# A two-layer decoder trunk: residual stream laid out by tokens, with weights as the moving operand of the output projections

## Chip, core and metric

The kernel runs on one core of one Trainium2 chip. The metric is the device time of one execution in microseconds (us). The engines are TensorE (PE in the profile, with PEld for its weight loads), VectorE (DVE), ScalarE (ACT), GpSimd (POOL) and SyncE (SP), whose queue issues the DMAs.

## What is computed

512 tokens of width 1024 go through two layers. Each layer has a token mixer (a gated DeltaNet in layer 0, forgetting attention, "fox", in layer 1), four heads of attention to 256 memory rows beside it, an output projection and a squared-ReLU MLP. Everything is float32.

```python
def rms_norm(x, w):
    y = x * lax.rsqrt(jnp.mean(x * x, axis=-1, keepdims=True) + EPS)
    return y * w
for i in range(2):
    h = rms_norm(x, norm1_w[i])
    mix, q_mem = gated_deltanet(h, ...) if i == 0 else forgetting_attention(h, ...)
    mem_out = memory_attention(q_mem, mem_k, mem_v, memq_norm_w[i])
    x = x + jnp.concatenate([mix, mem_out], axis=-1) @ w_out[i]      # 1536 -> 1024
    h = rms_norm(x, norm2_w[i])
    x = x + jnp.square(jax.nn.relu(h @ w_mlp1[i])) @ w_mlp2[i]       # 1024 -> 4096 -> 1024
```

In forgetting attention the projections q, k, v and gate are 1024 wide each (8 heads of 128); q and k are normalised per head.

## The kernel before

Every float32 operand of a large product is cut into a rounded part ("hi") and the rest ("lo"). `mm3` (L156 to L160) makes three products of them: hi hi, hi lo, lo hi. The weights come in slabs of 512 KB (1024 rows by 256 columns, or 512 rows by 512 columns): a DMA brings the raw slab, ACT casts it to the hi part (L297), DVE subtracts to get the lo part (L298). `prepare` does this some slabs ahead.

**Layout.** From the output projection of layer 0 on, the residual stream x is feature-major: 8 blocks of 128 features by 512 tokens (`x_blk`). `rows512` (L1278) makes x += w part for one slab of 512 weight rows and 512 columns: for each block of 128 output features 12 products, in which 128 weight columns are stationary and the 512 tokens of the input are the moving operand; then DVE adds the PSUM tile to the block of x (L1287). The output projection is three such groups (memory heads, then heads 0 to 3, then 4 to 7), the second half of the MLP eight.

**Norms.** Since x has features on partitions, the sum of squares of a token runs across partitions. For each finished block `split` (ACT L396, DVE L397) multiplies by the norm's weight and writes hi and lo of the next input hT at once, without the token's scale; `add_sq` squares the block (ACT L407) and POOL adds it to `sqs` (L408). After the last block, products of `ones` with `sqs` (L165) give the sums, twelve small DVE operations (L373, L208 to L212, L374) the rsqrt, and `r_row` spreads it along the free axis by 4 transposes (L170). So products on hT can start before the scale is known; the scale is applied when results leave PSUM: in the MLP's `hidden` (L1302, then the square on POOL L1303, the cast on ACT L1304, the lo part on DVE L1305), in the copies of layer 1's mixer (L1225, L467) and in the gate (L1248).

**MLP.** The hidden layer is 8 groups of 512. `m1(g, s)` makes 256 hidden columns from a slab (48 products with 512 tokens moving, `gemm_feat`). Groups alternate: m1(g, 0), half of the second product of group g-1, m1(g, 1), the other half.

**Layer 1's mixer.** First a 264-wide product (8 forget logits and 256 columns of memory queries, L1211), then four pairs of heads. For each pair k, q and v come by `gemm_tok2`: token-major tiles [128 tokens, 256], with hT as the stationary operand and 256 weight columns moving, 24 products for each of 4 tiles; the gate is feature-major (`gemm_feat`, 48 products of 512). k and q are normalised per head in the background (`group_scale`: POOL L444, DVE L445, DVE small operations, POOL L450; then transposes in `heads_T2`), and `self.drain("qk")` after the gate waits in the program for both.

**Order.** There is one instruction stream per engine, fixed when the program is built. Side work (norms, head attention) is written as generators in lanes; each `yield` says how much TensorE work in ns shall stand before the next step, and `pump` puts the steps between the products of the main stream. A `drain` emits the steps of a lane at once. Nothing is reordered on the chip: each engine works off its own list and waits on semaphores.

Of the kernel before, what the change touches and what calls it, by code (L numbers as in the profile page):

```python
# [7 lines left out]
F32 = mybir.dt.float32  # L8
# [22 lines left out]
# columns of the packed per-partition parameters  # L31
# [7 lines left out]
PC_N = 110  # L39
NPC = 134  # L40


class Kern:
# [68 lines left out]
    # A step yields how much TensorE work (in ns) goes before its results are used.  # L112
# [28 lines left out]
    def drain(self, *names, until=None):  # L141
        """Traces the lanes by their times until the named ones are at their ends, or until a mark is set."""
# [12 lines left out]
    def mm3(self, out, l, r, start, stop):  # L155
        """float32 product through the exact parts: hi hi + hi lo + lo hi."""  # L156
# [46 lines left out]
    def rsqrt(self, v, n):  # L203
        """v: AP [P, n] (with its guard added); returns v ** -0.5."""
# [10 lines left out]
    def log1p_half(self, u, n):  # L215
        """u in (0, 1]: log(1 + u) / 2 = atanh(u / (2 + u))."""
# [23 lines left out]
    def plan_weights(self):  # L240
# [42 lines left out]
    def prepare(self, n, cuts=1, also={}):  # L283
        """Splits slabs of the plan; if self.help, GpSimd takes half of the subtractions."""
# [20 lines left out]
    def slab(self, ahead=1):  # L305
        """The next slab of the plan: a function (k, columns) -> its hi and lo parts."""
# [11 lines left out]
    def gemm_feat(self, hT, evac, blk0=0, need=None):  # L318
        """Two feature-major blocks [128, 512] of hT's projection."""
# [10 lines left out]
    def gemm_tok(self, hT, evac, N=512, ns=2, nt=NT, by_tile=False, need=None):  # L330
        """Token-major [128, N] for each tile of tokens; ns slabs of 512 rows."""
# [3 lines left out]
        for s in range(1 if by_tile else ns):  # L335
            w = None if by_tile else self.slab()
            ks = range(K) if by_tile else range(4 * s, 4 * s + 4)
            order = [(k, t) for t in range(nt) for k in ks] if by_tile else [(k, t) for k in ks for t in range(nt)]
            for k, t in order:
                if need and (k if by_tile else t) == 0:  # L340
                    self.drain(until=need(t if by_tile else k))
# [5 lines left out]
    def gemm_tok2(self, hT, evac):  # L347
        """Token-major [128, 256] for each tile of tokens; one slab of 256 columns."""
        w = self.slab()
        for t in range(NT):  # L350
            ps = self.pacc()[:, :256]
            for k in range(KC):
                self.mm3(ps, hT(k, slice(t * P, t * P + P)), w(k), k == 0, k == KC - 1)
            evac(t, ps)
# [11 lines left out]
    def sq_sums(self, sqs, n, r):  # L366
        """r[:, i] = rsqrt(mean + eps) of the tokens of column block i of sqs [P, n * 128], summed over partitions."""
        nc = self.nc
        ps = self.paux3()
        for i in range(n):  # L370
            self.mm(ps[:, i], sqs[:, i * P:(i + 1) * P], self.ones)
        v = self.small(n)
        nc.vector.tensor_scalar(v, ps[:, :n, 0], 1.0 / D, EPS, ALU.mult, ALU.add)  # L373
        nc.vector.tensor_copy(r, self.rsqrt(v, n))  # L374

    def r_row(self, r):
        """The norm's scale of each token along the free axis, on all partitions; a generator."""
        nc = self.nc
        rb = self.scr3()
        nc.vector.tensor_copy(rb, self.bc(r, P))  # L380
        yield 1090.0
        ps = self.paux3()
        for t in range(NT):
            self.tr(ps[:, t], rb[:, t])
        self.rrow = self.cst.tile([P, T], F32, tag="rrow", name=self.nm("rrow"))
        nc.scalar.copy(self.rrow, ps.rearrange("p a b -> p (a b)"))

    def n_col(self, i, b):
        return self.par[:, PC_N + 8 * (i - 1) + b:PC_N + 8 * (i - 1) + b + 1]

    def split(self, hT, b, v, i):
        """v [P, T], times norm i's weight, into the parts of block b of hT."""
        nc = self.nc
        hi, lo = hT(b)
        w = self.n_col(i, b)
        nc.scalar.activation(hi, v, AF.Copy, scale=w)  # L396
        nc.vector.scalar_tensor_tensor(lo, v, w, hi.bitcast(F32), ALU.mult, ALU.subtract)  # L397

    def add_sq(self, b, xb):
        """Adds block b's squares to the norm's sums."""  # L400
        nc = self.nc
        if b == 0:
            self.sqs = self.cst.tile([P, T], F32, tag="sqs", name=self.nm("sqs"))
            nc.scalar.activation(self.sqs, xb, AF.Square)
        else:
            sq = self.scr()
            nc.scalar.activation(sq, xb, AF.Square)  # L407
            nc.gpsimd.tensor_add(self.sqs, self.sqs, sq)  # L408

    def norm_end(self, name):  # L410
        yield 2800.0
        self.r = self.cst.tile([P, NT], F32, tag="r", name=self.nm("r"))
        self.sq_sums(self.sqs, NT, self.r)
        self.marks.add("r" + name)
        yield 5520.0
        yield from self.r_row(self.r)
        self.marks.add("row" + name)
# [20 lines left out]
    def group_scale(self, raw, n, mult, eps):  # L438
        """raw [P, n, 128], scaled in place by rsqrt(mult * sum of squares + eps) of each group."""
# [13 lines left out]
    def heads_T(self, raw, dst, wcol, nt=NT):  # L453
        """raw [P, nt * 4, 128] (tile, head) -> dst [P, 4 heads, nt * 128], times a weight per row."""
# [8 lines left out]
    def cut2(self, parts, v, w):  # L463
        """v times a weight per row, into its hi and lo parts."""
# [4 lines left out]
    def heads_T2(self, raw, parts, wcol):  # L469
        """raw [P, 4 tiles * 2 heads, 128] -> the parts [P, 2 heads, T] of its transpose, times a weight per row."""  # L470
# [12 lines left out]
    def load_x(self, src):  # L483
        self.xs = [self.slot(T) for _ in range(2)]
        for b in range(0, KC, 2):
# [944 lines left out]
```

## Time and profile before

| | us |
|---|---|
| three runs | 1460.39, 1461.47, 1464.43 |
| their median | 1461.47 |
| span of the profiled execution | 1458.1 |
| PE busy in it | 1433.3 (98%) |
| DVE, ACT, POOL busy | 895.9, 584.1, 361.9 |

The span runs from the first to the last instruction; the median of the runs lies 3.4 us above it. A profile row of an engine's timeline gives start, duration, engine, line and operation, out<-in with shapes, and in brackets the idle time before it with what released it. Products overlap in the PE, so the distance from start to start says what one costs in a dense stream, not its duration.

### The profile page before, as it was taken

What the parts mean: (1) busy time and instruction counts of PE and PEld (TensorE: products, weight loads), DVE (VectorE), ACT (ScalarE), POOL (GpSimd) and SP (SyncE); (2) the same over time, 40 slices, a digit from 0 to 9 for tenths busy, and PEclk for the clock granted to TensorE, in tenths of its full rate; (3) what the DMA queues carried; (4) which work ended last, traced back from release to release, by engine and by line L of the source; (5) the groups of instructions that cost most, each with busy time, mean ns of one, the idle gap of its engine ahead of it and who ended that gap; (6) DMA issues with size and microseconds to landing.
All of it is one profiled execution on the core that took longest, in us unless ns stands there. A gap on an engine that the chain in (4) does not pass through costs nothing.

```text
span 1458.1 us, 20510 instructions
## 1 busy us (share of the span) xinstructions
PE 1433.3 (98%) x7886; PEld 1221.3 (84%) x7886; DVE 895.9 (61%) x1660; ACT 584.1 (40%) x1024; POOL 361.9 (25%) x406
## 2 busy tenths in 40 slices
PE   8999999989999999999999999999999999999999
PEld 6988777878888888888889999999888888888887
DVE  7689987577665554554566756657656545545544
ACT  7464655654342222222234554554534222222221
POOL 2274233223031111111122443444313101101100
PEclk9999999999999999999999999999999999999999
DMA  7541231232223223223335232213323322322331
GB/s 249 171 148 59 67 114 61 72 123 88 84 91 102 91 98 101 95 93 101 98 99 168 72 103 86 89 66 122 132 87 102 101 93 84 113 98 85 107 101 59
DMA packets 49783, 148.35 MB, mean 102 GB/s; under 512 B 5459, under 2 KB 10259, under 8 KB 49429
## 3 DMA queue, kind: packets, MB, share of 16 engines
q1 hardware_dynamic: 49536, 146.96, 30.8%
q8 instruction: 62, 1.02, 0.3%
q14 instruction: 37, 0.30, 0.1%
q10 hardware_dynamic: 148, 0.07, 0.0%
HBM read 139.64 MB, written 7.37 MB: 101 GB/s over the span
## 4 chain that ended last, share of the span: by engine, by line
PE 82%; DVE 9%; DMA 2%; ACT 2%; issue 2%; POOL 2%; ACTq 0%; SPq 0%; POOLq 0%; DVEq 0%
PE acc L158 25%; PE acc L159 24%; PE acc L160 24%; PE aux L165 3%; PE aux L170 2%; DVE wl L298 2%; DVE cv L751 2%; PE aux L160 1%; PE aux L158 1%; PE aux L159 1%; DVE slot L830 1%; ACT wh L297 1%; DMA t<-gd 1%; DVE slot L828 1%; POOL t L930 0%
## 5 line engine op out<-in xcount | busy, mean ns | idle before, releaser
L158 PE MATMUL acc<-slot,wh 128*128 128x512 f32 x1476 | 579.8, 393 | 0.0
L159 PE MATMUL acc<-slot,wh 128*128 128x512 f32 x1476 | 574.7, 389 | 0.3 <-DVE slot L1269 0.3
L160 PE MATMUL acc<-slot,wl 128*128 128x512 f32 x1476 | 574.4, 389 | 0.0
L297 ACT ACTIVATE wh<-wr 128x1024 fp32r<-128x1024 f32 (+3 forms) x242 | 247.6, 1025 | 494.4 <-PE acc L159 456.7
L298 DVE TENSOR_TENSOR wl<-wr,wh 128x1024 fp32r<-128x1024 f32 (+3 forms) x240 | 299.2, 1249 | 217.9 <-ACT wh L297 213.5
L160 PEld LDWEIGHTS acc<-slot,wl 128*128 128x128 f32 x1476 | 277.1, 188 | 57.7
L158 PEld LDWEIGHTS acc<-slot,wh 128*128 128x128 f32 x1476 | 277.2, 188 | 55.1
L159 PEld LDWEIGHTS acc<-slot,wh 128*128 128x128 f32 x1476 | 277.4, 188 | 54.7 <-DVE slot L1269 0.6
L1303 POOL TENSOR_TENSOR cv<-cv 128x512 f32<-128x512 f32 x64 | 94.7, 1501 | 536.7 <-DVE cv L1302 523.3
L158 PE MATMUL acc<-wh,slot 128*128 128x256 f32 (+3 forms) x608 | 187.7, 310 | 1.4 <-ACT slot L509 0.8
L159 PE MATMUL acc<-wl,slot 128*128 128x256 f32 (+3 forms) x608 | 183.8, 302 | 0.9 <-POOL wl L298 0.7
L160 PE MATMUL acc<-wh,slot 128*128 128x256 f32 (+3 forms) x608 | 182.9, 302 | 0.0
L1287 DVE TENSOR_TENSOR slot<-slot,acc 128x512 f32<-128x512 f32 x177 | 120.5, 681 | 96.1 <-PE acc L160 95.9
L158 PEld LDWEIGHTS acc<-wh,slot 128*128 128x128 f32 x608 | 116.3, 191 | 7.1 <-ACT slot L509 2.4
L159 PEld LDWEIGHTS acc<-wl,slot 128*128 128x128 f32 x608 | 116.4, 191 | 6.0 <-DVE wl L298 1.4
L160 PEld LDWEIGHTS acc<-wh,slot 128*128 128x128 f32 x608 | 115.9, 191 | 3.8
L1302 DVE SCALAR_TENSOR_TENSOR cv<-acc,rrow 128x512 f32<-128x512 f32 x64 | 43.7, 691 | 80.0 <-PE acc L160 80.0
L1305 DVE TENSOR_TENSOR slot<-cv,slot 128x512 fp32r<-128x512 f32 x64 | 69.7, 1090 | 6.9 <-ACT slot L1304 2.4
L1304 ACT CAST slot<-cv 128x512 fp32r<-128x512 f32 x64 | 39.8, 622 | 58.4 <-POOL cv L1303 58.4
L751 DVE SCALAR_TENSOR_TENSOR cv<-acc,par,cv 128x511 f32<-128x511 f32 (+2 forms) x72 | 51.4, 740 | 16.0 <-ACT cv L748 15.6
L408 POOL TENSOR_TENSOR sqs<-sqs,cv 128x512 f32<-128x512 f32 x21 | 28.8, 1369 | 108.8 <-ACT cv L407 108.8
L444 POOL TENSOR_TENSOR cv<-slot 128x512 f32<-128x512 f32 x26 | 31.0, 1197 | 57.8 <-ACT slot L1225 30.7
(249 smaller groups left out, 1348.7 us busy)
## 6 DMA issues: line engine op xcount, KB each, us to landing
wr<-in_w_mlp SPq DMA_DIRECT2D x128, 512.0 KB, 3.8
wr<-in_w_out SPq DMA_DIRECT2D x24, 512.0 KB, 4.3
wr<-in_dn_k SPq DMA_DIRECT2D x8, 512.0 KB, 4.8
wr<-in_dn_v SPq DMA_DIRECT2D x8, 512.0 KB, 4.6
wr<-in_dn_q SPq DMA_DIRECT2D x8, 512.0 KB, 3.6
wr<-in_dn_z SPq DMA_DIRECT2D x8, 512.0 KB, 4.0
wr<-in_fox_k SPq DMA_DIRECT2D x8, 512.0 KB, 4.1
wr<-in_fox_q SPq DMA_DIRECT2D x8, 512.0 KB, 3.7
```

The costliest lines, as they stand in the source:

```text
L158: mm(out, l[0], r[0], start=start, stop=False)
L159: mm(out, l[0], r[1], start=False, stop=False)
L160: mm(out, l[1], r[0], start=False, stop=stop)
L165: self.nc.tensor.matmul(out, l, r, start=start, stop=stop)
L297: nc.scalar.activation(hi[:, c], raw[i][:, c], AF.Copy)
L298: eng.tensor_sub(lo[:, c], raw[i][:, c], hi[:, c].bitcast(F32))
L751: nc.vector.scalar_tensor_tensor(y[:, s:], ps[:, :T - s], w(j), y[:, s:], ALU.mult, ALU.add)
L1287: self.nc.vector.tensor_add(xv, xv, ps)
L1302: nc.vector.scalar_tensor_tensor(r, ps, 0.0, self.rrow, ALU.max, ALU.mult)
L1303: nc.gpsimd.tensor_mul(r, r, r)
L1304: nc.scalar.copy(hh[:, b, :], r)
L1305: nc.vector.tensor_sub(hl[:, b, :], r, hh[:, b, :].bitcast(F32))
```

## The change

x becomes token-major: 4 tiles of 128 tokens by 1024 features (`x_tile`), and the output leaves the kernel that way. In the output projections and second MLP matrices (`tile_add`) 128 tokens of the input are stationary and 512 weight columns move. The last group of each takes both slabs and goes by pairs of tiles (`rows_last`), so that `norm_tile` can start on a tile when its 1024 features are there: two squares with a sum on ACT, 13 small DVE operations per tile, two DVE multiplications by scale and weight (in `transposed`), 8 PE transposes, ACT copies for hi and DVE subtractions for lo. hT now has the scale, so the evictions lose their multiplications; in `hidden` ACT does the ReLU and DVE the square. The first MLP group of each layer works on 2 slabs at once, in halves of 256 tokens (`gemm_halves`), the second half needing tiles 2 and 3. The 264-wide product of layer 1 goes by tiles. k and q of a pair come from one slab pair 512 wide, v for two pairs at once.

```diff
-                    pl += [a["fox_" + n][p] for p in (2 * g, 2 * g + 1) for n in "kqvg"]
+                    for p in (2 * g, 2 * g + 1):
+                        pl += tok(a["fox_kq"][p])
+                        if p % 2 == 0:
+                            pl += tok(a["fox_v"][g])
+                        pl += [a["fox_g"][p]]
...
+    def gemm_halves(self, hT, evac, need):
+        w = [self.slab(), self.slab(0)]
+        ps = [self.pacc() for _ in range(4)]
+        for i in range(2):
+            c = slice(256 * i, 256 * i + 256)
+            for t in range(2 * i, 2 * i + 2):
+                self.drain(until=need(t))
+            for j in range(2):
+                for k in range(KC):
+                    for b in range(2):
+                        self.mm3(ps[2 * j + b][:, c], w[j](k, slice(b * P, b * P + P)), hT(k, c), k == 0, k == KC - 1)
+        for b in range(4):
+            evac(b, ps[b])
...
+    def stats(self, tiles, r):
+        nc = self.nc
+        for i, xt in enumerate(tiles):
+            s2 = self.small(2)
+            for f in range(2):
+                jk = self.scr()
+                nc.scalar.activation(jk, xt[:, f * 512:(f + 1) * 512], AF.Square, accum_out=s2[:, f:f + 1])
+            nc.vector.tensor_add(r[:, i:i + 1], s2[:, 0:1], s2[:, 1:2])
+        nc.vector.tensor_scalar(r, r, 1.0 / D, EPS, ALU.mult, ALU.add)
+        nc.vector.tensor_copy(r, self.rsqrt(r, len(tiles)))
...
+    def norm_weight(self, i):
+        w = self.cst.tile([P, D], F32, tag="nw", name=self.nm("nw"))
+        self.nc.sync.dma_start(w, self.a["norms"][i].partition_broadcast(P))
+        return [w[:, g * 512:(g + 1) * 512] for g in range(2)]
+    def norm_tile(self, i, t, hT, w, spill=None):
+        yield 700.0
+        xt = self.x_tile(t)
+        r = self.small(1)
+        self.stats([xt], r)
+        if spill is not None:
+            self.nc.sync.dma_start(spill[t], xt)
+        yield 3600.0
+        yield from self.transposed(xt, w, r, hT.parts, t)
+        self.marks.add(f"h{i}{t}")
...
-        self.gemm_tok(hT, e0, N=264, need=lambda k: f"h2{k}")
+        self.gemm_tok(hT, e0, N=264, by_tile=True, need=lambda t: f"h2{t}")
...
+            def e(t, ps, rv=rv):
+                nc.scalar.copy(rv[:, :, t, :], ps.rearrange("p (j c) -> p j c", j=2))
+            self.gemm_tok(hT, e)
...
-                self.gemm_tok2(hT, e)
...
             if p % 2 == 0:
+                vh, vl = self.slot(512, F32R), self.slot(512, F32R)
+                def e(t, ps, vh=vh, vl=vl):
+                    nc.scalar.copy(vh[:, t, :], ps)
+                    nc.vector.tensor_sub(vl[:, t, :], ps, vh[:, t, :].bitcast(F32))
+                self.gemm_tok(hT, e)
                 gate = self.slot(T)
...
-                nc.vector.tensor_mul(gv, ps, self.rrow)
-                nc.scalar.activation(gv, gv, AF.Sigmoid)
+                nc.scalar.activation(gv, ps, AF.Sigmoid)
...
+    def tile_add(self, t, f, part, w, c=slice(0, 512)):
+        ps = self.pacc()[:, c]
+        for k in range(4):
+            self.mm3(ps, tuple(m[:, t * P:t * P + P] for m in part(k)), w(k, c), k == 0, k == 3)
+        xv = self.x_tile(t)[:, f * 512 + c.start:f * 512 + c.stop]
+        self.nc.vector.tensor_add(xv, xv, ps)
...
+    def rows_last(self, part, after, last=False):
+        w = [self.slab(), self.slab(0)]
+        for i in range(2):
             for f in range(2):
+                for t in (2 * i, 2 * i + 1):
+                    cut = [slice(0, 256), slice(256, 512)] if last and i and f and t % 2 else [slice(0, 512)]
+                    for c in cut:
+                        self.tile_add(t, f, part, w[f], c)
+                        if last:
+                            after(t, slice(f * 512 + c.start, f * 512 + c.stop))
+                    if f and not last:
+                        after(t)
...
-            nc.vector.scalar_tensor_tensor(r, ps, 0.0, self.rrow, ALU.max, ALU.mult)
-            nc.gpsimd.tensor_mul(r, r, r)
+            nc.scalar.activation(r, ps, AF.Relu)
+            nc.vector.tensor_mul(r, r, ps)
             nc.scalar.copy(hh[:, b, :], r)
             nc.vector.tensor_sub(hl[:, b, :], r, hh[:, b, :].bitcast(F32))
...
-        m1(0, 0, lambda k: f"h{name}{k}")
-        m1(0, 1)
+        self.gemm_halves(hT, lambda b, ps: hidden(0, b, ps), lambda t: f"h{name}{t}")
```

The built programs differ as follows: products 512 wide into `acc` go from 4692 to 5076, products 256 wide from 1368 to 600, PE transposes from 76 to 160 instructions of the kind aux<-ident,cv; POOL loses the 64 squares of `hidden` and the 21 additions to `sqs`.

**The order at two places.** In the rows, acc and aux are PSUM tiles, wh and wl the parts of a weight slab, wr the raw slab, cv a 2 KB scratch tile, sm small per-token numbers, nw the norm's weight, slot any 8 KB tile (x and hT among them); "x4" is four instructions of a kind.

VectorE at the end of the first output projection, before: the last addition to x (L1287), two lo parts of weights (L298), the last lo part of hT (L397).

```order
L1287 TENSOR_TENSOR slot_3424<-slot_3424,acc_4220 128x512
L397 SCALAR_TENSOR_TENSOR slot_3422<-slot_3424,par,slot_3420 128x512
L1287 TENSOR_TENSOR slot_3424<-slot_3424,acc_4239 128x512
L298 TENSOR_TENSOR wl_4259<-wr_4178,wh_4258 128x1024
L298 TENSOR_TENSOR wl_4263<-wr_4179,wh_4262 128x1024
L397 SCALAR_TENSOR_TENSOR slot_3422<-slot_3424,par,slot_3420 128x512
```

There and now, from the last addition to x (L1257) on; L301 is the weights' lo part now, L384, L385, L207, L209 to L211 and L386 the small operations of `stats`:

```order
L1257 TENSOR_TENSOR slot_3426<-slot_3426,acc_4271 128x512
L385 TENSOR_SCALAR sm_4288<-sm_4288 128x1
L301 TENSOR_TENSOR wl_4326<-wr_4321,wh_4325 128x1024
L207 TENSOR_SCALAR sm_4296<-sm_4288 128x1
L301 TENSOR_TENSOR wl_4330<-wr_4322,wh_4329 128x1024
L209 TENSOR_TENSOR sm_4297<-sm_4296 128x1
L210 SCALAR_TENSOR_TENSOR sm_4297<-sm_4297,sm_4288 128x1
L211 SCALAR_TENSOR_TENSOR sm_4296<-sm_4297,sm_4296 128x1
```

and at the end of this chain, behind six more of its operations:

```order
L384 TENSOR_TENSOR sm_4353<-sm_4354 128x1
L386 COPY sm_4288<-sm_4296 128x1
L385 TENSOR_SCALAR sm_4353<-sm_4353 128x1
L413 SCALAR_TENSOR_TENSOR cv_4392<-slot_3426,sm_4288,nw_3423 128x512
L207 TENSOR_SCALAR sm_4361<-sm_4353 128x1
L413 SCALAR_TENSOR_TENSOR cv_4394<-slot_3426,sm_4288,nw_3423 128x512
```

What was one operation on hT behind the last addition is now a chain: the first normalised half of tile 2 (cv_4392) comes 17 rows behind that addition, the halves of tile 3 (cv_4414, cv_4416) a dozen rows after tile 2's second.

TensorE where the first output projection ends, before: the last products on x (acc_4239), then the first of the MLP, 512 tokens wide.

```order
L158 MATMUL acc_4239<-slot_3463,wh_4092 128x512
L159 MATMUL acc_4239<-slot_3464,wh_4092 128x512
L160 MATMUL acc_4239<-slot_3463,wl_4093 128x512
L158 MATMUL acc_4270<-slot_3419,wh_4170 128x512
L159 MATMUL acc_4270<-slot_3421,wh_4170 128x512
L160 MATMUL acc_4270<-slot_3419,wl_4171 128x512
```

The same stretch now, 51 products of 256 behind the last product on x (acc_4339 and acc_4340 are PSUM tiles of `gemm_halves`):

```order
L157 MATMUL acc_4340<-slot_3419,wh_4325 128x256
L158 MATMUL acc_4340<-slot_3421,wh_4325 128x256
L159 MATMUL acc_4340<-slot_3419,wl_4326 128x256
L169 MATMUL aux_4424<-ident,cv_4392 128x128 x4
L157 MATMUL acc_4339<-slot_3419,wh_4325 128x256
L158 MATMUL acc_4339<-slot_3421,wh_4325 128x256
L159 MATMUL acc_4339<-slot_3419,wl_4326 128x256
L169 MATMUL aux_4434<-ident,cv_4394 128x128 x4
```

The transposes of tile 2 now stand 54 products of 256 behind the last product on x, those of tile 3 another 12 products behind tile 2's second group; before, no transposes of x stood here. At the start of layer 1's mixer the same transposes stand 48 products of 264 (tile 2) and 50 to 56 of them (tile 3) behind the last product on x.

## Rows read from the trace of the kernel before

**Rows 1.** Profile page, busy time by engine: us, share of the span, instructions.

```profile
PE 1433.3 (98%) x7886; PEld 1221.3 (84%) x7886; DVE 895.9 (61%) x1660; ACT 584.1 (40%) x1024; POOL 361.9 (25%) x406
```

**Rows 2.** Busy time by stretch: us, then PE, PEld, DVE, ACT, POOL; PEclk granted clock.

```profile
0.00:350.00 350.00, 330.24 (x2123) 272.37 (x2124) 270.29 (x647) 203.83 (x422) 122.75 (x158) 1.00 0.36 117
...
420.00:766.00 346.00, 345.92 (x1533) 286.23 (x1532) 182.40 (x211) 93.97 (x110) 55.52 (x38) 1.00 0.30 99
766.00:782.00 16.00, 15.39 (x126) 15.06 (x125) 8.80 (x25) 7.28 (x18) 2.57 (x2) 1.00 0.42 138
782.00:1016.00 234.00, 233.28 (x1754) 223.77 (x1753) 149.27 (x367) 121.94 (x240) 97.02 (x132) 1.00 0.30 96
...
1108.00:1458.00 350.00, 346.50 (x1545) 287.02 (x1543) 176.17 (x204) 84.11 (x93) 48.65 (x33) 1.00 0.29 95
300.00:305.00 5.00, 2.28 (x11) 1.55 (x11) 4.76 (x11) 2.27 (x4) 3.56 (x3) 1.00 0.00 0
```

**Rows 3.** Waits of PE from 350 us to the end: total, times, longest.

```profile
PE aux L170 <- POOL t L665: 0.7, 1, 0.7
PE aux L165 <- ACT t L999: 0.7, 1, 0.7
PE acc L158 <- DVE slot L1287: 0.6, 1, 0.6
```

**Rows 4.** PE's timeline: products 512 wide, start to start.

```profile
763.66 0.39 PE L160 MATMUL acc<-slot,wl 128*128 128x512 f32 x1
763.89 0.39 PE L158 MATMUL acc<-slot,wh 128*128 128x512 f32 x1
```

**Rows 5.** PE's timeline in the fox stage: products 256 wide.

```profile
800.03 0.28 PE L158 MATMUL acc<-wh,slot 128*128 128x256 f32 x1
800.15 0.28 PE L159 MATMUL acc<-wl,slot 128*128 128x256 f32 x1
```

**Rows 6.** PE's timeline: four transposes between products.

```profile
36.16 0.63 PE L170 MATMUL aux<-ident,cv 128*128 128x128 f32 x4 [1.30 <-DVE cv L426]
36.55 0.37 PE L158 MATMUL acc<-wh,slot 128*128 128x272 f32 x1
36.76 0.29 PE L159 MATMUL acc<-wl,slot 128*128 128x272 f32 x1
```

**Rows 7.** PE's timeline: the sums over partitions of one norm.

```profile
421.69 1.16 PE L165 MATMUL aux<-ones,sqs 128*128 128x128 f32 x8
422.60 0.47 PE L158 MATMUL acc<-slot,wh 128*128 128x512 f32 x1
422.92 0.39 PE L159 MATMUL acc<-slot,wh 128*128 128x512 f32 x1
```

**Rows 8.** PE's timeline at the start of layer 1's mixer.

```profile
767.81 0.28 PE L159 MATMUL acc<-wl,slot 128*128 128x264 f32 x1
768.71 0.39 PE L158 MATMUL acc<-wh,slot 128*128 128x264 f32 x1 [0.61 <-DVE slot L1287]
```

**Rows 9.** DVE's timeline: the rsqrt of one norm, first and last of its twelve.

```profile
772.93 0.16 DVE L373 TENSOR_SCALAR sm<-aux 128x4 f32<-128x4 f32 x1 [0.98 <-PE aux L165]
...
775.10 0.17 DVE L374 COPY r<-sm 128x4 f32<-128x4 f32 x1
```

**Rows 10.** Groups of DVE's instructions by line: busy us, mean ns, idle before.

```profile
L298 DVE TENSOR_TENSOR wl<-wr,wh 128x1024 fp32r<-128x1024 f32 x220 | 281.7, 1283 | 206.1 <-ACT wh L297 201.9 <-PE aux L170 2.2 <-PE aux L165 1.6
L1287 DVE TENSOR_TENSOR slot<-slot,acc 128x512 f32<-128x512 f32 x175 | 119.7, 684 | 94.4 <-PE acc L160 94.1
L445 DVE TENSOR_REDUCE sm<-cv 128x4 f32<-128x512 f32 x26 | 17.2, 678 | 4.1 <-POOL cv L444 4.1
L467 DVE SCALAR_TENSOR_TENSOR slot<-aux,par,slot 128x512 fp32r<-128x512 f32 x20 | 14.7, 745 | 2.1 <-ACT slot L466 1.9
```

**Rows 11.** Groups of POOL's instructions by line, the scaling of q and k.

```profile
L450 POOL TENSOR_TENSOR slot<-slot,sm 128x512 f32<-128x512 f32 x26 | 31.1, 1218 | 26.3 <-DVE sm L212 22.6 <-DVE sm L1153 2.1 <-DVE sA L796 1.2
L444 POOL TENSOR_TENSOR cv<-slot 128x512 f32<-128x512 f32 x26 | 31.0, 1197 | 57.8 <-ACT slot L1225 30.7 <-ACT slot L1210 20.7 <-ACT slot L753 4.6
```

More of the change, by code (lines that the diff above doesn't have):

```diff
@@ L336, in gemm_tok @@
             w = None if by_tile else self.slab()
-            ks = range(K) if by_tile else range(4 * s, 4 * s + 4)
-            order = [(k, t) for t in range(nt) for k in ks] if by_tile else [(k, t) for k in ks for t in range(nt)]
+            ks = range(4 * s, 4 * s + 4)
+            order = ([(4 * j + k, 2 * i + t) for i in range(nt // 2) for j in range(ns) for t in range(2) for k in range(4)]
+                     if by_tile else [(k, t) for k in ks for t in range(nt)])
             for k, t in order:
-                if need and (k if by_tile else t) == 0:
-                    self.drain(until=need(t if by_tile else k))
+                if need and k == 0:
+                    self.drain(until=need(t))
                 self.mm3(ps[t], hT(k, slice(t * P, t * P + P)), (ws[k // 4] if by_tile else w)(k % 4),
@@ L345, in gemm_tok @@
                     evac(t, ps[t])
[L347 to L354, printed above, removed]
+    def gemm_halves(self, hT, evac, need):
[4 more added lines that the diff above has]
+            for t in range(2 * i, 2 * i + 2):
+                self.drain(until=need(t))
+            for j in range(2):
[4 more added lines that the diff above has]
+            evac(b, ps[b])
     def new_hT(self):
@@ L363, in new_hT @@
         return get
-    def sq_sums(self, sqs, n, r):
+    def stats(self, tiles, r):
         nc = self.nc
[L369 to L408, printed above, removed]
@@ L483, in load_x @@
     def load_x(self, src):
[L484 to L489 removed]
+        self.xs = [self.slot(D) for _ in range(2)]
+        for t in range(NT):
+            self.nc.sync.dma_start(self.x_tile(t), src[t])
     def memory(self):
@@ L539, in memory @@
         krw = self.slot(HD)
-        def stats(tiles, r):
-            for i, xt in enumerate(tiles):
-                s2 = self.small(2)
-                for f in range(2):
-                    jk = self.tmp()
-                    nc.scalar.activation(jk, xt[:, f * 512:(f + 1) * 512], AF.Square, accum_out=s2[:, f:f + 1])
-                nc.vector.tensor_add(r[:, i:i + 1], s2[:, 0:1], s2[:, 1:2])
-            nc.vector.tensor_scalar(r, r, 1.0 / D, EPS, ALU.mult, ALU.add)
-            nc.vector.tensor_copy(r, self.rsqrt(r, 2))
         def x_norm(i, start):
             yield start
-            stats([self.x_tile(2 * i + j) for j in range(2)], rx[i])
+            self.stats([self.x_tile(2 * i + j) for j in range(2)], rx[i])
             yield 3450.0
@@ L563, in mem_r @@
             yield 9230.0
-            stats([mt[:, t, :] for t in range(2)], rm)
+            self.stats([mt[:, t, :] for t in range(2)], rm)
         self.spawn("norm", x_norm(0, 5000.0))
@@ L1273, in out_proj, with rows512 @@
             part = (lambda k: (mh[:, k, :], ml[:, k, :])) if grp is None else self.mix[grp]
-            for f in range(2):
-                self.rows512(part, f, after if n == 2 else None)
-    def rows512(self, part, f, after, last=False):
-        w = self.slab()
-        for b in range(4):
-            cols = [slice(0, T)] if not (last and b == 3) else [slice(0, 256), slice(256, T)]
-            for c in cols:
-                ps = self.pacc()[:, c]
-                for k in range(4):
-                    self.mm3(ps, w(k, slice(b * P, b * P + P)), tuple(m[:, c] for m in part(k)), k == 0, k == 3)
-                xv = self.x_blk(4 * f + b)[:, c]
-                self.nc.vector.tensor_add(xv, xv, ps)
-                if after:
-                    after(4 * f + b, c)
+            if n < 2:
+                self.rows512(part)
+            else:
+                self.rows_last(part, after)
+    def tile_add(self, t, f, part, w, c=slice(0, 512)):
[4 more added lines that the diff above has]
+        self.nc.vector.tensor_add(xv, xv, ps)
+    def rows512(self, part, fs=(0, 1)):
+        for f in fs:
+            w = self.slab()
+            for t in range(NT):
+                self.tile_add(t, f, part, w)
+    def rows_last(self, part, after, last=False):
+        w = [self.slab(), self.slab(0)]
+        for i in range(2):
+            for f in range(2):
+                for t in (2 * i, 2 * i + 1):
[6 more added lines that the diff above has]
+                        after(t)
     def mlp(self, hT, name, after):
@@ L1317, in mlp @@
                 m1(g, f)
-                self.rows512(part(g - 1), f, None)
-        for f in range(2):
-            self.rows512(part(7), f, after, name == "3" and f)
+                self.rows512(part(g - 1), (f,))
+        self.rows_last(part(7), after, name == "3")
     def run(self):
```

83 lines of the change are left out of this document (29 added, 54 removed).

## The prediction, as put on record

> **What bounds the kernel now.** I read the page first: PE is busy for 1433.3 of 1458.1 us [rows 1], so the end is set by PE's own work and by the few places where PE stands. Where these are, the busy time by stretch tells [rows 2]: in the first 350 us (memory keys, DeltaNet) PE lacks 19.8 us, and behind them hardly anything: 0.1 us in the 346 us of the first MLP, 0.6 in the 16 us where layer 1 begins, 0.7 in the fox stage, 3.5 in the last stretch, behind the last product as far as no wait is listed. The list of PE's waits agrees: from 350 us on three waits of 0.6 to 0.7 us [rows 3]. Two things follow. What the change saves on DVE, ACT or POOL (DVE has 182 busy us in the 346 us of the first MLP [rows 2]) buys nothing, since PE waits for none of them there. And each us by which the change adds to PE's stream, or by which it makes PE wait where it waits for nothing now, shows in full. The change lies almost wholly behind 350 us; in front of it the parts shared with it (statistics of the first norm) keep their instructions, and I cost them at nothing, by up to 1 us either way.
>
> The sum is made against the profiled execution, 1458.1 us; the median of the runs, 1461.5, lies 3.4 us above it, and I add these at the end. About 0.3% (4.4 us) is what a measurement of this kernel can tell from no change.
>
> **PE's work.** Prices are from start to start. A 512-wide product costs 0.23 us, over a longer run of them 0.227 [rows 4]; a 256-wide one 0.12 [rows 5]. That both operands change places in the output projections and second MLP products costs nothing by this: the same number of 512-wide products stays, only weights move now instead of tokens.
> - Fox slabs: k, q and v are 4 pairs x 3 slabs x 96 = 1152 products of 256, 138.2 us; 576 products of 512 take 130.8. **-7.4 us**, in a stage where PE is full (233.28 of 234 us [rows 2]), so it counts.
> - First MLP group in halves: 96 products of 512 per layer become 192 of 256. 192 x 0.227 = 43.6 us become 384 x 0.12 = 46.1. **+2.5**.
> - Transposes: four took 0.39 us, and the first product behind them 0.21 instead of 0.12 [rows 6], so 0.48 for four. The 3 norms now transpose 4 tiles x 8 = 32 each, 96; the 12 of the scale's row go. 84 more, 21 x 0.48 = **+10.1**.
> - Sums over partitions: eight products took 0.91 us and the next one 0.32 instead of 0.23 [rows 7]; three norms, **-3.0**.
>
> PE's work alone grows by 2.2 us.
>
> The Trainium skill (TensorE: Matmul & The Clock Gate, "Back-to-back issue gap") states a sustained spacing of 81 ns at 128 columns and 131 ns at 512. By it 256 columns would be about 98 ns, an estimate between the two, and the fox slabs would gain 37 us and the halves lose 12. The rows show 230 and 120 ns in the dense stream [rows 4, 5], so the measurement decides, and the sum goes by it.
>
> **The norms' ends.** This is the part that I am least sure of and that the sign hangs on. Before, a block of hT is ready one ACT and one DVE operation after its addition, and the scale follows while PE is 5 us and more into the next products; only at the mixer's start does PE wait, 0.61 us [rows 8]. Now a tile's transposes need its statistics first. At the end of an output projection the order of DVE gives, behind the last addition: the addition itself 0.68, two lo parts of weights 1.28 each [rows 10], fourteen small operations, a multiplication like L467 of 0.75 [rows 10], and the second half of tile 2 is another small one and 0.75 later. Small operations that depend on each other went at (775.10 - 772.93) / 11 = 0.197 us [rows 9]. So the halves of tile 2 are ready at 0.68 + 2.56 + 2.76 + 0.75 = 6.8 and 7.7 us. PE is at their transposes after 54 x 0.12 = 6.5 us: it waits about 0.5 us in front of the first (with 0.2 for the signal), 0.4 in front of the second. Tile 3's first half is ready ten small operations, a lo part of hT and a multiplication later, at 11.1 us, the second at 11.9; PE gets there 12 products later, at 9.6, waits 1.6, and then 0.5. Together 3.0 us. If DVE is 0.8 us behind already when the addition comes, it is 4; if its operations follow each other as closely as some do, 2.2. I take **3 us, twice** (layers 0 and 1).
>
> At the mixer's start the 264-wide product (0.12 us each [rows 8]) is worked off by tiles: 48 products, 5.9 us, cover tile 2, and tile 3's transposes stand right behind those of tile 2. The weights' lo parts are half as wide there and the two tiles' chains interleave; by the same count tile 3 is ready at 8 to 8.8 us, while PE is there at 6.8, and the first product on each tile must still wait for ACT and DVE to put hi and lo into hT. 1.5 to 3 us, I take **2**, less the 0.8 us gap there now (768.71 - 767.81 is 0.90 for one product of 0.12 [rows 8]). The norms' ends: 3 + 3 + 2 - 0.8 = **+7.2**. Not below 0 for each, since a wait can't give back; at most 4 + 4 + 3.
>
> **The fox stage's drains.** For each pair the program waits, behind the gate's 48 products (10.9 us), for k and q to be scaled and transposed. Now k and q come together from one slab pair. For pairs 0 and 2, v's 96 products (21.8 us) stand in between; for pairs 1 and 3 only the gate's. The chain: two squares on POOL for each of k and q, 4 x 1.20, their scaling 4 x 1.22 [rows 11], DVE's reductions of 0.68 [rows 10], some twelve small operations (2.4), transposes, ACT and DVE at the end (about 2): 12 to 16 us as POOL's pieces overlap or not. Before, q had 22.4 us of products behind it (v's 96 of 256 and the gate's). What stands in the order between (the previous pair's attention, its scores and transposes) covers part; I take **+1.5** for the two odd pairs together, from 0 to 6.
>
> **Nothing, with its cover.** `hidden` moves a square from POOL to DVE and a ReLU to ACT, with the same number of steps, and 24 products of 512 (5.4 us) lie ahead of its use; without that cover each step would add its half microsecond or so to each of the 14 later groups, which no wait before hints at [rows 3]. Three broadcasts of the norm's weight and four spills of x in place of eight run on SP's queue, its share 0.30 [rows 2], ahead of the slabs; a late slab would show as a wait of PE's weight loads for DVE's lo part, which doesn't occur now behind 350 us [rows 3]. The gate loses a multiplication.
>
> **Sum.** 1458.1 + 2.2 + 7.2 + 1.5 = 1469.0; with 3.4 us above the span 1472.4, and as the terms carry half a microsecond each I say **1472**.
>
> **Rivals.**
> - *The chains are hidden* (the other side, not slower). If tile 2 is ready within 6.5 us of the last product on x, and tile 3 within 9.2, PE doesn't stop: then only the work counts, and 0.8 us of old gap goes, 1461.5 + 1.4 = 1463, no change that can be measured. For it: DVE is idle for half of the first MLP [rows 2], and small operations of two tiles interleave at the mixer. Against: DVE's order at the boundary is full, and small operations take 0.2 us each whatever they do [rows 9]. It decides at each boundary on some 0.3 to 2 us, and would have to hold at all three.
> - *Odd pairs' k and q uncovered*: at two drains PE stands for 3 to 5 us each rather than 0.8: +5 to +9 more, 1477 to 1482. For it: 10.9 us of gate against 12 to 16. Against: the previous pair's attention is in the order there, and PE lost 0.7 us in the stage before [rows 2].
> - *PE's clock falls at the boundaries.* A wait of 2 us and transposes together make a stretch with few real products. The row that speaks: from 300 to 305 us PE worked 2.28 of 5 us, and the granted clock was 1.00, the full 2.4 GHz, there and everywhere [rows 2]. If it fell to 1.2 GHz behind each boundary for the remaining 40 products of the first half, 256-wide ones taking twice 0.12, that is some 5 us each: 1487. The Trainium skill (same page, "Part 4: PE-mode transpose") says that transposes don't count as busy time for the clock; by the trace's rows I give this little.
> - *Faster*: the merged slabs gain more than the difference of the two spacings, because the weight loads halve too; a load has a mean of 0.155 us (1221.3 / 7886 [rows 1]), more than the 0.12 of a 256-wide product. Full cover of the norms and 6 us more from the fox stage would give 1457. Against: loads run beside products, and the stage's spacing of 0.12 already holds them [rows 5]. The page's rule on spacing, named above, would act in this direction, by up to 20 us.
>
> **How the numbers follow.** Waits of a few us at the boundaries, with work +2 (my case, 1467 to 1478): 0.62. Chains hidden, 1461.5 to 1465.5: 0.15. Odd pairs uncovered, 1477 to 1482: 0.13. Clock or late slabs, beyond 1482: 0.05. Faster: 0.05. The range 1463 to 1481 takes in the first case whole, two thirds of the second and most of the third: about 0.8. Faster by over 0.3% (under 1457.1): 0.05; within 0.3% (to 1465.9): 0.15; slower: 0.80.
>
> **What the profile will show.** PE's waits: at the end of each output projection and at the mixer's start, lines of 0.3 to 2 us, PE for aux of L169 released by DVE's cv of L413, some 8 us in all; none before. The fox stage shorter by about 7 us of products, with waits at the third and first pair's drain. Transposes aux<-ident,cv up to 160. If the list of waits from 350 us on stays under 3 us in all, the forecast is wrong by the waits; if a 512-wide product with weights moving isn't 0.227 us from start to start, it is wrong by the work; if fox doesn't get shorter, by that term.

## The result, and the profile after

1475.05 us, median of 4 runs (1474.05 to 1476.7), against 1460.93 of before (4 runs): ratio 1.0092, interval 1.0077 to 1.0107. Slower, some 14 us, and inside the range; but the time was not lost where the forecast put most of it. The profiled execution has a span of 1474.9 us, 16.8 more than the one of before; it was the slowest of the four.

Page and busy time by stretch (columns as in [rows 1] and [rows 2]):

```profile
PE 1442.8 (98%) x7562; PEld 1210.6 (82%) x7562; DVE 875.2 (59%) x1785; ACT 606.2 (41%) x1087; POOL 241.9 (16%) x321
```

```profile
0.00:350.00 350.00, 329.70 (x2115) 273.33 (x2116) 269.87 (x646) 202.69 (x420) 123.72 (x158) 1.00 0.37 118
...
420.00:770.00 350.00, 349.28 (x1645) 293.33 (x1644) 172.27 (x256) 108.42 (x147) 0.00 (x0) 1.00 0.31 98
770.00:790.00 20.00, 19.99 (x151) 18.85 (x150) 16.69 (x50) 11.56 (x30) 0.00 (x0) 1.00 0.61 208
790.00:1025.00 235.00, 232.50 (x1194) 195.81 (x1193) 139.11 (x330) 117.25 (x216) 94.57 (x127) 1.00 0.30 96
1025.00:1120.00 95.00, 91.10 (x435) 75.30 (x434) 62.76 (x152) 39.44 (x74) 19.04 (x33) 0.96 0.29 95
```

From 420 to 790 us PE is nearly as full as before: 0.7 us are missing in the first MLP (0.1 before), none at the mixer's start. It lacks 2.5 us in the fox stage and 3.9 in the 95 us behind it, where the granted clock is 0.96 (before, 0.7 us were missing in the fox stage, at a clock of 1.00 [rows 2]). The list of PE's waits from 350 us on answers to [rows 3]:

```profile
PE aux L169 <- POOL t L1130: 3.9, 3, 2.8
PE aux L169 <- DVE cv L413: 1.4, 2, 0.7
PE aux L169 <- POOL slot L437: 1.4, 2, 0.8
PE aux L169 <- DVE t L1150: 0.9, 1, 0.9
PE aux L164 <- ACT t L973: 0.7, 1, 0.7
```

L413 is the norms' ends: 1.4 us in two waits, where 8 us were forecast. L437 (scaling of q and k), L1130 (the last step of a head's softmax) and L1150 (the lo part of its transpose) are the fox stage: 6.2 us. PE's timeline at the last pair's drain shows what they cost:

```profile
1028.78 0.93 PE L169 MATMUL aux<-ident,t 128*128 128x128 f32 x7
...
1031.64 0.63 PE L169 MATMUL aux<-ident,slot 128*128 128x128 f32 x4 [0.93 <-DVE t L1150]
...
1037.76 0.39 PE L159 MATMUL aux<-slot,slot 128*128 128x512 f32 x1
1040.91 0.47 PE L169 MATMUL aux<-ident,t 128*128 128x128 f32 x1 [2.77 <-POOL t L1130]
1041.04 0.77 PE L157 MATMUL acc<-wh,slot 128*128 128x512 f32 x1
1041.61 0.63 PE L158 MATMUL acc<-wl,slot 128*128 128x512 f32 x1
...
1046.73 0.74 PE L159 MATMUL acc<-wh,slot 128*128 128x512 f32 x2
1047.31 0.40 PE L157 MATMUL acc<-wh,slot 128*128 128x512 f32 x1
```

From 1028.8 us PE has no product of a slab until 1041: it works off the end of the previous pair's attention, the transposes of k and q (one wait of 0.93 us) and the scores of this pair's first head, and then waits 2.77 us for that head's softmax. Behind this wait the 512-wide products are 0.43 us apart until 1047.3: 15 products in 6.27 us, which take 3.4 at 0.227, so 2.9 us more. The granted clock of these stretches:

```profile
1040.00:1045.00 5.00, 4.09 (x10) 3.25 (x11) 4.02 (x11) 3.46 (x10) 0.85 (x2) 0.52 0.57 231
1045.00:1050.00 5.00, 5.00 (x19) 4.06 (x18) 1.24 (x4) 0.82 (x2) 0.59 (x1) 0.80 0.00 0
```

0.52 is the lower level (1.2 GHz) for nearly all of the stretch. Added up from start to start, less the dense price of each product and transpose, PE lost 8.4 us between 1025 and 1050 and 3.5 us between 925 and 950 (the second pair's drain); before, 0.2 and 0.0.

### The profile page after: what moved, and what is told of

Its sections match the earlier page's. It is cut to its first block, busy times and chain, and to the rows that moved or that the text cites. A ratio compares the mean times of both kernels' runs of the same rounds, so it can differ in the third digit from the quotient of the medians.

```text
span 1474.9 us, 19902 instructions
## 1 busy us (share of the span) xinstructions
PE 1442.8 (98%) x7562; PEld 1210.6 (82%) x7562; DVE 875.2 (59%) x1785; ACT 606.2 (41%) x1087; POOL 241.9 (16%) x321
## 4 chain that ended last, share of the span: by engine, by line
PE 82%; DVE 12%; POOL 2%; issue 1%; DMA 1%; ACT 1%; ACTq 0%; SPq 0%; POOLq 0%; DVEq 0%
PE acc L157 25%; PE acc L159 24%; PE acc L158 24%; PE aux L164 3%; PE aux L169 3%; DVE wl L301 2%; DVE cv L725 1%; DVE cv L413 1%; PE aux L159 1%; PE aux L157 1%; PE aux L158 1%; DVE sm L210 1%; DVE slot L804 1%; DVE sm L211 1%; DVE slot L802 1%
## 5 line engine op out<-in xcount | busy, mean ns | idle before, releaser
L157 PE MATMUL acc<-wh,slot 128*128 128x512 f32 (+3 forms) x1124 | 433.1, 386 | 1.2 <-ACT slot L493 1.2
L301 DVE TENSOR_TENSOR wl<-wr,wh 128x1024 fp32r<-128x1024 f32 (+3 forms) x240 | 290.5, 1211 | 237.7 <-ACT wh L300 234.9
L158 PE MATMUL acc<-wl,slot 128*128 128x512 f32 (+3 forms) x1124 | 427.2, 380 | 0.7 <-POOL wl L301 0.7
L159 PE MATMUL acc<-wh,slot 128*128 128x512 f32 (+3 forms) x1124 | 425.8, 380 | 0.0
L300 ACT ACTIVATE wh<-wr 128x1024 fp32r<-128x1024 f32 (+3 forms) x242 | 247.9, 1025 | 390.3 <-PE acc L159 219.5
L157 PE MATMUL acc<-slot,wh 128*128 128x512 f32 (+1 forms) x832 | 315.0, 379 | 0.0
L159 PE MATMUL acc<-slot,wl 128*128 128x512 f32 (+1 forms) x832 | 311.6, 375 | 0.0
L158 PE MATMUL acc<-slot,wh 128*128 128x512 f32 (+1 forms) x832 | 311.4, 374 | 0.0
L157 PEld LDWEIGHTS acc<-wh,slot 128*128 128x128 f32 x1124 | 213.1, 190 | 39.1 <-ACT slot L493 2.8
L159 PEld LDWEIGHTS acc<-wh,slot 128*128 128x128 f32 x1124 | 212.5, 189 | 39.3
L158 PEld LDWEIGHTS acc<-wl,slot 128*128 128x128 f32 x1124 | 213.0, 190 | 36.9 <-POOL wl L301 1.0
L1257 DVE TENSOR_TENSOR slot<-slot,acc 128x512 f32<-128x512 f32 x177 | 120.4, 680 | 119.9 <-PE acc L159 119.8
L159 PEld LDWEIGHTS acc<-slot,wl 128*128 128x128 f32 x832 | 157.0, 189 | 27.7
L157 PEld LDWEIGHTS acc<-slot,wh 128*128 128x128 f32 x832 | 157.1, 189 | 26.6
L158 PEld LDWEIGHTS acc<-slot,wh 128*128 128x128 f32 x832 | 157.3, 189 | 26.1
L1291 DVE TENSOR_TENSOR cv<-cv,acc 128x512 f32<-128x512 f32 x64 | 43.4, 684 | 94.4 <-ACT cv L1290 94.4
L1290 ACT ACTIVATE cv<-acc 128x512 f32<-128x512 f32 x64 | 37.7, 595 | 114.7 <-PE acc L159 114.7
L1293 DVE TENSOR_TENSOR slot<-cv,slot 128x512 fp32r<-128x512 f32 x64 | 43.7, 688 | 2.5
```

What stands on the lines that cost most here:

```text
L157: mm(out, l[0], r[0], start=start, stop=False)
L158: mm(out, l[0], r[1], start=False, stop=False)
L159: mm(out, l[1], r[0], start=False, stop=stop)
L300: nc.scalar.activation(hi[:, c], raw[i][:, c], AF.Copy)
L301: eng.tensor_sub(lo[:, c], raw[i][:, c], hi[:, c].bitcast(F32))
L1257: self.nc.vector.tensor_add(xv, xv, ps)
```

## The experiments

All ratios are to the kernel before, run on the same chip beside them.

**1. Fox slabs as before, all else changed.** `self.gemm_tok(hT, e)` of k and q, and of v for two pairs, becomes three `gemm_tok2` per pair:

```diff
-                    for p in (2 * g, 2 * g + 1):
-                        pl += tok(a["fox_kq"][p])
-                        if p % 2 == 0:
-                            pl += tok(a["fox_v"][g])
-                        pl += [a["fox_g"][p]]
+                    pl += [a["fox_" + n][p] for p in (2 * g, 2 * g + 1) for n in "kqvg"]
```

> Undoes the fox slabs alone: k, q and v of each pair by 256-wide slabs as before, all the rest as in the changed kernel (1475 us). Theory 'drains' (PE's new waits are those for k and q of the odd pairs, some 12 us with the slower products behind the last one): the waits go, 7.4 us of products come back, 1470 to 1471 us, and from 350 us on PE waits for little but the two norms' ends (0.7 us each). Theory 'norms' (the forecast: 7 us at the norms' ends, 1.5 in the drains): 1475 + 7.4 - 1.5 = 1481 us.

Measured: 1470.82 us, 1.0067 (1.0054 to 1.008). This is what 'drains' had forecast, and 10 us below 'norms'. PE's waits from 350 us on (L417 is the norms' multiplication here):

```profile
PE aux L169 <- DVE cv L417: 1.5, 2, 0.8
PE aux L164 <- ACT t L977: 0.7, 1, 0.7
PE aux L169 <- POOL t L643: 0.2, 1, 0.2
```

The fox waits are gone. What is left over before, 9.8 us by the ratio, is the token-major part: by the forecast's own prices 10.1 (transposes) + 2.5 (halves) - 3.0 (sums) + 1.8 (two norms' ends, 0.9 each from start to start) - 0.8 = 10.6.

**2. Only v by pair again.**

```diff
-                        if p % 2 == 0:
-                            pl += tok(a["fox_v"][g])
-                        pl += [a["fox_g"][p]]
+                        pl += [a["fox_v"][p], a["fox_g"][p]]
```

> k and q stay 512 wide, v is made per pair by a 256-wide slab again, so that each pair has v's 96 products (11.5 us) and the gate's 48 (10.9 us) behind k and q. Theory 'drains': the 12 us of waits go, products grow by 2.5 us: 1465 to 1466 us. Theory 'norms': 1475 + 2.5 - 1.5 = 1476 us.

1468.71 us, 1.0063 (1.0051 to 1.0075): the direction of 'drains', 3 us short of it. PE's longest fox wait is 0.4 us; the loss between 750 and 1050 us is 4.3 instead of 14.6 us. By the traces 10.3 - 2.5 = 7.8 us are gained over the changed kernel, by the runs 4 to 6. In the profile the difference is the first stage, which that execution left 1.6 us later; what holds the other executions above the expectation stays open.

**3. The first stage.** Its stage ended 2.5 us later in the profile after than before, which the forecast had at nothing.

```diff
-                jk = self.scr()
+                jk = (tile or self.scr)()
```

For x and the memory `tile` is `self.tmp`, the pool of before.

> The first statistics (rows of x and of the memory) put their squares into the pool of before again, all the rest as in the changed kernel. Theory 'early order' (the shared pool of scratch tiles holds up the first norm, 2.5 to 4 us in the first 75 us): 1471 to 1473 us, and PE's wait near 36 us for the normalised x goes from 2.5 to about 1.3 us. Theory 'chance' (the profiled run only started later): 1475 us.

1476.39 us, 1.0104 (1.0088 to 1.012): the time is that of 'chance'. PE's wait for the normalised x, 2.5 us in one piece in the change, was 2.5 us in two. The kernel of run 4, whose first stage is that of before to the letter, came to the same product at 350.8 us, against 348.6 before and 351.1 after; run 9, whose first stage is the changed kernel's, came to it as early as before:

```profile
348.50 0.39 PE L159 MATMUL acc<-wh,slot 128*128 128x512 f32 x1
```

So the 2 us are between executions. In the one after, the granted clock was 0.74 from 65 to 70 us and 0.92 in the next 5 us, where before it was 1.00.

**4. The fox slabs alone, on the kernel before.** (the edit of run 1 the other way round, and v for two pairs)

> The other way round: the kernel before (1461 us) with the fox slabs of the change alone (k and q 512 wide, v 512 wide for two pairs). Theory 'drains': 1461 - 7.4 + 12 = 1465 to 1466 us, with waits for POOL and DVE in the third and last drain. Theory 'norms': 1461 - 7.4 + 1.5 = 1455 us.

1467.94 us, 1.0056 (1.0044 to 1.0068). The slabs meant to save 7.4 us cost 8.2, the direction of 'drains' and some 2 to 4 us more than it said:

```profile
PE aux L170 <- POOL slot L454: 4.0, 2, 2.7
PE aux L170 <- DVE t L1180: 3.0, 1, 3.0
```

In this profile the granted clock fell behind both drains, to 0.50 between 930 and 935 us and to 0.57 between 1030 and 1035. From start to start PE lost 6.0 us between 925 and 950 and 7.5 between 1025 and 1050.

**5 and 6. k and q of both pairs first, then v, then both gates.** In the changed kernel, and alone in the kernel before:

```diff
-                    for p in (2 * g, 2 * g + 1):
-                        pl += tok(a["fox_kq"][p])
-                        if p % 2 == 0:
-                            pl += tok(a["fox_v"][g])
-                        pl += [a["fox_g"][p]]
+                    pl += tok(a["fox_kq"][2 * g]) + tok(a["fox_kq"][2 * g + 1]) + tok(a["fox_v"][g])
+                    pl += [a["fox_g"][2 * g], a["fox_g"][2 * g + 1]]
```

> The changed kernel with its fox slabs 512 wide, but in another order: k and q of both pairs of a group, then v, then the two gates, so that even the odd pair has v's and two gates' products (43.6 us) behind its k and q. No product more than in the changed kernel (1475 us; 1.0092 of before). Theory 'drains' (it is the cover, not the width): the 12 us of waits and slower products go, 1463 to 1465 us, 1.001 to 1.004 of before. Rival 'width' (512-wide k and q make the chain itself late wherever they stand): 1470 us or more.

> The kernel before with the same order of 512-wide fox slabs as in the run ahead, and nothing else of the change. Theory 'drains': the 7.4 us of products are gained and no wait is added, 1452 to 1454 us, 0.994 to 0.996 of before. Rival 'width': no gain, 1459 us or more.

1475.29 us, 1.0106 (1.009 to 1.0121), and 1464.55 us, 1.0039 (1.0025 to 1.0053): 'drains' missed both, and by the times the rival 'width' holds (1470 or more, 1459 or more). The traces don't show its mechanism: the waits at the drains did go (at most 0.2 us lost between 925 and 950, and between 1025 and 1050). Instead one wait of 4.2 us (4.1 in run 6) stood 45 us later, in front of the output projection's third group, which needs the last pair's attention; the granted clock behind it in run 5, busy time by stretch:

```profile
PE aux L169 <- POOL t L1127: 4.2, 1, 4.2
```

```profile
1085.00:1090.00 5.00, 2.32 (x8) 1.83 (x8) 2.43 (x14) 2.62 (x8) 4.07 (x10) 0.58 0.01 3
1090.00:1095.00 5.00, 5.00 (x21) 3.73 (x20) 0.82 (x2) 1.24 (x3) 0.30 (x1) 0.74 0.00 0
```

k and q of the odd pair were early, but the even pair's attention now waited for its gate, behind all the slabs; the last head's scores stood at 1081 us in run 5's trace, against 1075 in the change's. My theory was too narrow: what must be covered is not k and q but everything from the slab to the end of the last head's softmax.

**7. Every transpose of the norms twice** (on the kernel of run 1).

```diff
-            for k in range(4):
-                self.tr(ps[:, k], xn[g][:, k * P:(k + 1) * P])
+            for k in range(4 * n):
+                self.tr(ps[:, k % 4], xn[g][:, k % 4 * P:(k % 4 + 1) * P])
```

`n` is 2 in `norm_tile` and 1 elsewhere.

> On the kernel of the first experiment (fox slabs 256 wide, 1.0067 of before): each of the 96 transposes of the three norms is made twice. By the price of 0.0975 to 0.12 us each, 9.4 to 11.5 us more, 1.013 to 1.0145 of before. Rival (transposes ride in gaps of PE, and the 9.8 us of the first experiment come from elsewhere): no change, 1.0067.

1478.4 us, 1.013 (1.0114 to 1.0146): 9.2 us over run 1 by the two ratios (7 by the medians) for 96 transposes, about 0.1 each, with PE's waits at the norms' ends gone. So transposes don't ride in gaps.

**8. The first MLP group by 512 tokens** (on the kernel of run 1).

```diff
-        self.gemm_halves(hT, lambda b, ps: hidden(0, b, ps), lambda t: f"h{name}{t}")
+        for t in range(NT):
+            self.drain(until=f"h{name}{t}")
+        m1(0, 0)
+        m1(0, 1)
```

> On the same kernel: the first MLP group of each layer by 512 tokens as before (needs all four tiles' norms before its first product) instead of in halves. Work falls by 2.5 us, but nothing covers the chain of tiles 2 and 3, some 10 us from the last addition at each of two boundaries. Theory 'halves cover the chain': +15 to +18 us, 1.017 to 1.019 of before. Rival (the halves cover nothing, their cost is only work): -2.5 us, 1.005.

1490.63 us, 1.0213 (1.0199 to 1.0227), 21 us over run 1 and some 3 more than expected: 16.7 us of waits, and the clock. The waits, then the stretch with the second norm's end:

```profile
PE aux L169 <- DVE sm L207: 12.1, 2, 6.1
PE aux L169 <- DVE cv L417: 4.6, 2, 2.3
```

```profile
1125.00:1130.00 5.00, 1.38 (x7) 1.40 (x8) 4.58 (x21) 0.25 (x1) 0.00 (x0) 0.70 0.69 222
1130.00:1135.00 5.00, 2.68 (x12) 2.07 (x11) 3.62 (x11) 1.67 (x4) 0.00 (x0) 0.50 0.02 7
1135.00:1140.00 5.00, 5.00 (x18) 4.00 (x18) 1.02 (x2) 0.46 (x1) 0.00 (x0) 0.77 0.01 3
```

This is the bare chain of two tiles, 8.4 us at each norm's end, that the halves hide for 1.25 us of extra products.

**9 to 11. No drain.** The wait in the program goes; a pair's attention starts when its q is in the order:

```diff
     def fox_pair(self, p):
+        while f"qk{p}" not in self.marks:
+            yield 780.0
...
+                    if j:
+                        self.marks.add(f"qk{p}")
...
-            self.drain("qk")
```

Run 9 is the changed kernel with it, run 10 that of run 4, run 11 the kernel before with k and q merged and v by pair.

> The changed kernel with the wait for k and q behind each pair's gate taken out of the program: the pair's attention starts once their steps are in the order, and the products that follow (the next slabs, the output projection) stand between them. No product more or less. The last head's softmax now stands just ahead of the projection's third group, with some 25 products around it instead of 70. Theory 'cover' (drains, as the run with both pairs' k and q first has narrowed it: the chain of attention needs a fixed time behind the last slab, and PE waits for what of it no product covers): the waits of the third pair go, of the last pair's some 4 us stay in front of the third group, 1466 to 1468 us, 1.004 to 1.006 of before. Rival 'total' (the waits only move): 1475 us, 1.0092.

> The kernel before with the change's 512-wide fox slabs (1.0056 of before with the drain) and no drain. Theory 'cover': 7.4 us of products gained, 3 to 5 us of wait at the last head: 1456 to 1458 us, 0.997 to 0.999. Rival 'total': 1468 us.

> The kernel before with only k and q merged to 512 columns (v stays 256 wide per pair) and no drain. 768 products of 256 become 384 of 512, 92.2 to 87.2 us, -5.0 us; v's products stay behind k and q of every pair and 21 more 512-wide products stand behind the last head's scores than in the run ahead. Theory 'cover': at most 1 to 2 us of wait left, 1455 to 1457 us, 0.9965 to 0.9985, the fastest of all. Rival 'total': 1460 us or more.

1470.53 us, 1.0074 (1.006 to 1.0087); 1462.32, 1.0013 (1.0003 to 1.0023); 1456.89, 0.9976 (0.9966 to 0.9987). Run 10 is clearly faster than its kernel with the drain (1.0056), so the waits don't merely move; run 9 (1.0092 with it) is so by less than the intervals tell for sure. Both stay 2 to 6 us above their expectation. In run 9's profile the softmax costs 2.7 us in three waits, a little less than expected; its six executions had mean clocks from 1.000 down to 0.996, and the time goes roughly with them, from 1468 (the profiled one, inside the expectation) to 1473 us. What else there is in it stays open. Run 10's profile has the softmax and a second wait that no theory counted, for the norm's squares on POOL, which the kernel before doesn't have [rows 3] and run 6 has too (2.6 us):

```profile
PE aux L170 <- POOL t L1160: 2.6, 3, 1.3
PE aux L165 <- POOL sqs L412: 2.2, 1, 2.2
```

Run 11 came out as expected and beats both kernels, the one before by some 3 us and the change by some 17. It also speaks against 'width': k and q are 512 wide in it, and PE waits for neither. What taking out the drain alone gives the kernel before was not run; its fox stage lacked 0.7 us of PE to begin with [rows 2]. Run 11's waits from 350 us on, and its fox stage:

```profile
PE aux L165 <- ACT t L1000: 0.7, 1, 0.7
PE acc L158 <- DVE slot L1291: 0.6, 1, 0.6
PE acc L159 <- DVE slot L1273: 0.5, 1, 0.5
```

```profile
783.00:1013.00 230.00, 230.00 (x1374) 204.05 (x1373) 144.57 (x342) 119.96 (x220) 93.82 (x127) 1.00 0.31 100
```

## Why the prediction came out, point by point

The time was forecast as 1472 and came as 1475, by two errors of opposite sign: that it came so near is luck. With the work taken from the forecast's sum and the rest from the trace, the 16.8 us between the two spans are: work +2.2, the norms' ends +1.0, the fox drains 11.7 (8.4 + 3.5 - 0.2, slow products among them), and some 2 in the first stage that runs 3, 4 and 9 put down to chance. The sign that was set (under 3 us of waits behind 350 us would be wrong) was met with 8.5 us, but only 1.4 of them stood where it looked for them.

**PE's work, +2.2: right.** Weights as the moving operand keep the spacing (0.23 us from 413.51 to 413.74 and to 413.96), so the swap costs nothing by itself, and the sum by the rows held. Four transposes now take 0.35 us, and the next product 0.09 more, 0.44 instead of 0.48:

```profile
413.51 0.39 PE L159 MATMUL acc<-wh,slot 128*128 128x512 f32 x1
413.74 0.39 PE L157 MATMUL acc<-wh,slot 128*128 128x512 f32 x1
413.96 0.39 PE L158 MATMUL acc<-wl,slot 128*128 128x512 f32 x1
414.19 0.39 PE L159 MATMUL acc<-wh,slot 128*128 128x512 f32 x1
414.42 0.60 PE L169 MATMUL aux<-ident,cv 128*128 128x128 f32 x4
414.77 0.47 PE L157 MATMUL acc<-wh,slot 128*128 128x512 f32 x1
415.09 0.39 PE L158 MATMUL acc<-wl,slot 128*128 128x512 f32 x1
```

By this the transposes cost 9.2 instead of 10.1, and the work grows by 1.3 to 2.2. Run 7 confirms the price; run 1 the sum of the token-major part.

**The norms' ends, +7.2: mis-sized, it was +1.0.** The term was right in kind (run 8 has the chain uncovered) but three of its pieces were too long. DVE's timeline at the first norm's end; the first 256-wide product of the MLP started at 421.0:

```profile
421.43 0.68 DVE L1257 TENSOR_TENSOR slot<-slot,acc 128x512 f32<-128x512 f32 x1
...
424.41 0.15 DVE L209 TENSOR_TENSOR sm<-sm 128x1 f32<-128x1 f32 x1
...
425.96 0.16 DVE L211 SCALAR_TENSOR_TENSOR sm<-sm,sm 128x1 f32<-128x1 f32 x1
426.04 0.15 DVE L384 TENSOR_TENSOR sm<-sm 128x1 f32<-128x1 f32 x1
426.15 0.15 DVE L386 COPY sm<-sm 128x1 f32<-128x1 f32 x1
426.22 0.15 DVE L385 TENSOR_SCALAR sm<-sm 128x1 f32<-128x1 f32 x1
426.34 0.75 DVE L413 SCALAR_TENSOR_TENSOR cv<-slot,sm,nw 128x512 f32<-128x512 f32 x1
```

The small operations were priced at 0.197 each, all fourteen. That holds where one needs the last (eight steps in 1.55 us, 424.41 to 425.96); those of two tiles that alternate are 0.07 to 0.12 apart. From start to start the addition took 0.6 and a lo part 1.14, not their durations of 0.68 and 1.28. So tile 2's first half was ready at 427.1, 6.1 us behind 421.0 and not 6.8, and PE's transposes at 427.49 waited for nothing; tile 3's waited 0.7 us, once per output projection, and at the mixer PE waited for no norm. The rival 'chains are hidden' was nearer to this part than the forecast.

**The fox drains, +1.5 (0 to 6): this step failed, it was about 12.** I priced the chain (12 to 16 us behind 10.9 of cover) and then let "what stands in the order between" cover the rest. At the last pair that is the scores and the softmax of a head, which themselves wait for POOL and DVE: no cover but a second chain (1028 to 1041 above). Runs 1 and 4 show this part alone, by taking it out and by putting it in. The rival with the odd pairs uncovered had the place and, with 1.5 + 5 to 9 us, nearly the size; at 0.13 it was rated too low.

**The clock.** Given little, and put at the norms' ends; it fell behind the last drain, for 2.9 us. In run 8, with 6 us of wait at each norm's end, it fell there, to 0.50. In run 7, with twice the transposes and no wait, it stayed at 1.00:

```profile
420.00:430.00 10.00, 10.00 (x71) 9.19 (x70) 9.57 (x27) 5.76 (x11) 0.00 (x0) 1.00 0.40 135
```

So in these runs waits went ahead of the fall, and transposes among dense products did not bring it. That is no test of the Trainium skill's sentence that transposes don't count as busy time (TensorE: Matmul & The Clock Gate, "Part 4: PE-mode transpose"): products stood between them throughout.

**What had no weight** was so: POOL lost 120 us of work, and run 1's sum leaves no gain for it.

## What to carry to other kernels

When PE is full, a wider slab is worth the products that it saves only if the products that go were covering nothing: name the chain that begins at each slab and count what stands behind it, up to the last consumer, before merging. A stream of side work that itself waits is not cover. And a wait that is taken away at one drain (run 5) has to be looked for at the next one.

## What the runs showed of the hardware that I had not expected

The same wait is followed by a lower clock in some executions and not in others. Near 305 us each of these kernels has a wait of 2.7 to 2.8 us. In the profiled executions before [rows 2], after, and of runs 6 and 9 PE went on at 1.00; in the other nine the granted clock fell. Run 1 shows, behind 2.77 us at 307.4:

```profile
305.00:310.00 5.00, 2.62 (x17) 2.59 (x18) 4.67 (x12) 1.32 (x2) 1.04 (x1) 0.87 0.01 3
310.00:315.00 5.00, 5.00 (x34) 4.83 (x33) 1.85 (x7) 1.17 (x9) 0.81 (x1) 0.79 0.75 210
```

The spread of a kernel with such waits goes with it: run 3 took 1470.62 us in the execution with a mean clock of 1.000, and 1474.9 to 1477.6 in those at 0.997 to 0.998. Run 11, without waits of that length behind 350 us, has five of nine executions within 2 us of each other.

Also, `hidden`'s lo part on DVE took 1.09 us on average before (L1305) and 0.69 now (L1293), with the same operands and POOL's square beside it gone; that POOL was the cause was not tried, and as PE doesn't wait for it, it gained nothing.
